# Low parts of weights by a negated copy and an accumulating DMA

## The chip, the core and the metric

The kernel runs on one core of a Trainium2 chip. Its engines run side by side, each with its own queue of instructions, and wait for each other by semaphores: TensorE (PE, with its weight loads PEld), VectorE (DVE), ScalarE (ACT), GpSimd (POOL), and SyncE (SP), which here issues nearly all DMAs. The metric is the device time of one execution in microseconds (us).

## What is computed

One layer of a decoder in float32: 512 tokens with 16 meta tokens ahead of them (528 rows of width 1024). An attention mixer with an indexer that keeps the 128 best keys of each query, a residual with LayerNorm, a SwiGLU feed-forward of width 2816, and a second residual with LayerNorm:

```
proj = h @ w_in                      # q, k, v, indexer
... top-k keys of each query, 16 heads of softmax attention ...
h = layer_norm(alpha*h + out @ w_o, ln1)
ffn = (silu(h @ w_gate) * (h @ w_up)) @ w_down
h = layer_norm(alpha*h + ffn, ln2)
```

The output is h without the meta rows.

## The kernel before

**High and low parts.** PE multiplies in a format with fewer bits than float32. So each float32 operand x is written as hi + lo: hi is x rounded by a ScalarE copy (line 156), lo = x - hi a subtraction (line 159), and a product takes three matmuls, hi·hi, hi·lo and lo·hi (`mm3`, lines 286 to 288; for the down and output weights lines 1063 and 771). Weights are cut so at run time, in chunks of 128 x 1024 (512 KB).

**Chunks.** A chunk passes through three kinds of buffer of three each (`CHUNKS`): raw (`r_wq`, `r_wg`, ...: where SP's load lands), high (`h_...`) and low (`l_...`). `load` issues the DMA, `cut` issues the copy and the subtraction, `chunk` fetches the two parts for the matmuls, and `ahead(name)` cuts the next chunk of the list and loads the two after it. The lists are `g_in` (indexer), `g_qk` (wq0, wk0, ... wq7, wk7, wo0 to wo3, wr0 to wr3) and `g_ff` (wg0, wu0, ... wg21, wu21, then the down chunks wd).

**Late chunks.** `cut(..., late=True)` doesn't issue the subtraction at once but owes it in two pieces: columns 0 to 639 to VectorE, the rest to GpSimd. `settle` issues what is owed, at fixed places of a head, or when `chunk` wants the chunk. Late are fourteen chunks: wq3 to wq7, wk3 to wk7, wo0 to wo2 (cut by `stream`) and wo3. For gate and up, the gate's subtraction is on VectorE and the up's on GpSimd (wg0's is on GpSimd too), the down's on VectorE.

**Order.** The program order of each engine is that of the code. After the indexer and the top-k search comes a loop over the 16 attention heads. In a head stand the scores (`a1S` and so on, lines 313 and 314), VectorE's masked logits with the bias (line 653), ScalarE's exponentials (line 661), GpSimd's normalisation (line 670) and the bias additions for the next head (line 644, `bm`), PE's transposes (line 696), and the products with the values (line 726). Between them `fill` spends a budget of microseconds on pieces of the projections of later heads (`p_q`, `p_k`, lines 286 to 288) and, at the end, of the output projection (line 771). At the end of a head, and twice more within head 0, `stream` cuts the next weight chunk and loads ahead. Then come the first LayerNorm (lines 933 to 976), gate and up (line 991 on: 24 matmuls of 512 columns for each chunk, `p_wg` and `p_wu`), the down product (line 1037 on) and the second LayerNorm.

Of the kernel before, what the change touches and what calls it, by code (L numbers as in the profile page):

```python
# [11 lines left out]
F32 = mybir.dt.float32  # L12
F32R = mybir.dt.float32r
AF = mybir.ActivationFunctionType
ALU = mybir.AluOpType
# [35 lines left out]
AHEAD = 2  # L51
# [66 lines left out]
def trunk(ctx, tc, a, out):  # L118
    nc = tc.nc
# [8 lines left out]
    def unit(name, dt=F32, tag="u"):  # L128
        return up.tile([P, UNIT], dt, name=name, tag=tag, bufs=UNITS[tag])
# [25 lines left out]
    def act_copy(o, i, scale=1.0):  # L155
        nc.scalar.activation(o, i, AF.Copy, scale=scale)  # L156

    def sub(eng, o, x, y):
        eng.tensor_tensor(out=o, in0=x, in1=y.bitcast(F32), op=ALU.subtract)  # L159
# [21 lines left out]
    loaded, split, owed = {}, {}, []  # L181

    def load(group, i):
        if i < len(group):
            nm, src, n, _ = group[i]
            if nm not in loaded:
                loaded[nm] = raw(f"r_{nm}")[:, :n]
                nc.sync.dma_start(loaded[nm], src)

    def cut(group, i, late=False):  # L190
        if i < len(group):
            nm, _, n, eng = group[i]
            if nm not in split:
                load(group, i)
                hi = wp.tile([P, 1024], F32R, name=f"h_{nm}", tag="whi", bufs=CHUNKS[1])[:, :n]
                lo = wp.tile([P, 1024], F32R, name=f"l_{nm}", tag="wlo", bufs=CHUNKS[2])[:, :n]
                act_copy(hi, loaded[nm])
                split[nm] = (hi, lo)
                if late:
                    for e, c0, c1 in ((nc.vector, 0, SHARE), (nc.gpsimd, SHARE, n)):  # L200
                        owed.append((e, lo[:, c0:c1], loaded[nm][:, c0:c1], hi[:, c0:c1]))
                else:
                    sub(ENG[eng], lo, loaded[nm], hi)
# [7 lines left out]
    def chunk(name):  # L211

        group, i = where[name]
        if name not in split:
            cut(group, i)
        settle()
        return split[name]

    def ahead(name, late=False):
        group, i = where[name]  # L220
        cut(group, i + 1, late)
        for j in range(2, AHEAD + 2):
            load(group, i + j)

    def rows_load(name, src, tag="u"):
# [13 lines left out]
    g_in, g_qk, g_ff = groups  # L239
# [121 lines left out]
    for k in range(KT):  # L361
# [10 lines left out]
        if k == 0:  # L372
            load(g_in, 2)
    cut(g_in, 2)
    load(g_in, 3)
    for i, (t0, t1) in enumerate(HALF):
# [185 lines left out]
    def pair(p):  # L562

        pq = bank(f"p_q{p}", "mm")
        steps = project(f"wq{p}", NM, T, pq)
        using[0] = f"wq{p}"
        if p < 2:
            ahead(f"wq{p}")
        for k, _ in enumerate(steps):
            if k < KT - 1:  # L570
                yield 0.65
        Q2[2 * p], Q2[2 * p + 1] = queries(pq, -0.125, [f"q{2 * p + j}" for j in range(2)])
        yield 0.65
        ka = [unit(f"ka{2 * p + j}", F32R, "kq") for j in range(2)]
        for i, (t0, t1) in enumerate(HALF):
            pk = bank(f"p_k{p}_{i}", "mm")
            steps = project(f"wk{p}", t0, t1, pk[:, :264])
            if i == 0:
                using[0] = f"wk{p}"
                if p < 2:  # L580
                    ahead(f"wk{p}")
            for k, _ in enumerate(steps):
                if k < KT - 1:
                    yield 0.33
            keys(pk, t0, t1, *ka)
            if i:
                for j in range(2):
                    KA[2 * p + j], KB[2 * p + j] = ka[j], swapped(ka[j], f"kb{2 * p + j}")
            yield 0.33
# [39 lines left out]
    repeat(16)  # L629
    early(1)  # L630
    ahead("wk1")
    repeat(32)
    cut(g_qk, where["wk2"][1])
# [357 lines left out]
    for f in range(NF):  # L991
# [14 lines left out]
        if f < 8:  # L1006
            if f % 4 == 0:
                hq.append((quad(f"hh{f}", S), quad(f"hl{f}", S)))
            hi, lo = (x[:, f % 4] for x in hq[f // 4])
        else:  # L1010
            hi, lo = unit(f"hh{f}", F32R)[:, :S], unit(f"hl{f}", F32R)[:, :S]
# [25 lines left out]
    for th in range(2):  # L1037
# [9 lines left out]
        for f, o in steps:  # L1047
# [7 lines left out]
            else:  # L1055
                wh, wl = last[f - NF + TAIL]
                if th == 0 and o == outs[0] and f < NF - 1:
                    i = where["wd1_0"][1] + f - NF + TAIL
# [11 lines left out]
            su, n = done[b]  # L1070
# [74 lines left out]
```

## Time and profile before

| | |
|---|---|
| median of 3 runs | 689.28 us (687.64 to 690.19) |
| profiled execution | 688.74 us, its span 687.0 us |
| PE, PEld busy | 97%, 82% of the span |
| DVE, ACT, POOL busy | 61%, 42%, 36% |
| DMA | 83.11 MB, mean 121 GB/s |

Stages in the span: to about 50 us the indexer's projections, to 130 the top-k search beside projections, to 280 the attention heads, to 312 the output projection and first LayerNorm, to 556 gate and up, then the down product and its LayerNorm. Engines overlap, so an engine's busy time counts only where another engine waits for it; a matmul's own duration is modelled and longer than the distance to the next one.

### The profile page before, as it was taken

The numbers are of one execution on the slowest core, as the hardware profiler recorded it, in microseconds if no ns is written. First come the engines' busy times: TensorE is split into PE (matmuls) and PEld (weight loads), VectorE is DVE, ScalarE is ACT, GpSimd is POOL, SyncE is SP. The second block draws the span as 40 slices with busy tenths as digits, with TensorE's granted clock in tenths as the row PEclk, the third lists the DMA queues.
The fourth block names the chain that finished last, engine by engine and source line by source line (L and its number), as shares of the span: only waits on it lengthen the run. The fifth ranks groups of instructions, "written<-read, shape, count | busy, mean of one in ns | idle before, by whom it ended". The sixth has DMA issues, their size and how long they took to land.

```text
span 687.0 us, 9443 instructions
## 1 busy us (share of the span) xinstructions
PE 668.5 (97%) x3440; PEld 564.2 (82%) x3440; DVE 418.3 (61%) x788; ACT 287.6 (42%) x516; POOL 244.8 (36%) x249
## 2 busy tenths in 40 slices
PE   7999999999999999999999999999999999999995
PEld 5888787888998888888888888888888888888884
DVE  5589897898888887686334233343433355575425
ACT  5573512567767675513323233232322344423310
POOL 2063802597786776654212122221212200011004
PEclk9999999999999999999999999999999999999998
DMA  6557131542223245410131322313132267745601
GB/s 235 172 167 253 42 75 37 153 139 79 71 85 109 71 135 189 154 61 29 65 122 62 124 80 104 119 66 123 63 121 90 94 231 234 238 148 198 208 32 61
DMA packets 31806, 83.11 MB, mean 121 GB/s; under 512 B 3744, under 2 KB 8912, under 8 KB 31760
## 3 DMA queue, kind: packets, MB, share of 16 engines
q1 hardware_dynamic: 31328, 82.12, 36.6%
q8 instruction: 27, 0.44, 0.3%
q10 hardware_dynamic: 432, 0.39, 0.2%
q14 instruction: 19, 0.16, 0.1%
HBM read 74.86 MB, written 5.27 MB: 117 GB/s over the span
## 4 chain that ended last, share of the span: by engine, by line
PE 85%; DVE 6%; POOL 3%; ACT 2%; issue 2%; DMA 1%; SPq 0%; POOLq 0%; DVEq 0%; ACTq 0%
PE pd L1063 17%; PE p_wu L287 6%; PE p_wu L286 6%; PE p_wu L288 6%; PE p_wg L287 6%; PE p_wg L286 6%; PE p_wg L288 6%; PE po L771 3%; PE av L726 3%; PE pv L288 2%; PE pv L286 2%; PE pv L287 2%; PE pt L696 2%; PE p_q L288 2%; PE p_q L287 2%
## 5 line engine op out<-in xcount | busy, mean ns | idle before, releaser
L159 POOL TENSOR_TENSOR l_wu<-r_wu,h_wu 128x1024 fp32r<-128x1024 f32 x22 | 52.9, 2405 | 179.5 <-ACT h_wu L156 179.5
L1005 DVE TENSOR_TENSOR sg<-p_wu,sg 128x512 f32<-128x512 f32 x22 | 15.2, 692 | 107.6 <-PE p_wu L288 107.6
L159 DVE TENSOR_TENSOR l_wd<-r_wd,h_wd 128x1024 fp32r<-128x1024 f32 x36 | 45.4, 1263 | 41.2 <-ACT h_wd L156 41.1
L287 PE MATMUL p_wg<-h1l,h_wg 128*128 128x512 f32 (+1 forms) x184 | 70.0, 380 | 0.3 <-DVE h1l L159 0.3
L286 PE MATMUL p_wg<-h1h,h_wg 128*128 128x512 f32 (+1 forms) x184 | 70.0, 381 | 0.0
L286 PE MATMUL p_wu<-h1h,h_wu 128*128 128x512 f32 (+1 forms) x184 | 70.0, 380 | 0.0
L288 PE MATMUL p_wu<-h1h,l_wu 128*128 128x512 f32 (+1 forms) x184 | 69.9, 380 | 0.0
L287 PE MATMUL p_wu<-h1l,h_wu 128*128 128x512 f32 (+1 forms) x184 | 69.9, 380 | 0.0
L288 PE MATMUL p_wg<-h1h,l_wg 128*128 128x512 f32 (+1 forms) x184 | 69.9, 380 | 0.0
L159 DVE TENSOR_TENSOR l_wg<-r_wg,h_wg 128x1024 fp32r<-128x1024 f32 x21 | 52.9, 2518 | 24.4 <-ACT h_wg L156 24.4
L156 ACT ACTIVATE hh<-sg 128x512 fp32r<-128x512 f32 x22 | 13.9, 633 | 119.7 <-DVE sg L1005 119.7
L670 POOL TENSOR_TENSOR lg<-lg,rec 128x144 f32<-128x144 f32 (+1 forms) x64 | 52.6, 846 | 21.9 <-DVE rec L668 21.1
L1063 PE MATMUL pd<-h_wd,hh 128*128 128x512 f32 (+1 forms) x162 | 59.6, 368 | 0.0
L1063 PE MATMUL pd<-h_wd,hl 128*128 128x512 f32 (+1 forms) x162 | 59.6, 368 | 0.0
L1063 PE MATMUL pd<-l_wd,hh 128*128 128x512 f32 (+1 forms) x162 | 59.5, 368 | 0.0
L156 ACT ACTIVATE h_wd<-r_wd 128x1024 fp32r<-128x1024 f32 x36 | 38.1, 1061 | 45.6 <-DMA r_wd<-in_wd 23.2
L644 POOL TENSOR_TENSOR bm<-score,tz 128x256 f32<-128x256 f32 (+1 forms) x64 | 43.9, 717 | 16.4 <-DVE mn L653 14.9
L938 POOL TENSOR_TENSOR fr<-fr,half_neg 128x1 f32<-128x1 f32 x4 | 4.0, 992 | 116.0 <-DVE fr L937 116.0
L661 ACT ACTIVATE lg<-lg,mn 128x272 f32<-128x272 f32 (+1 forms) x64 | 36.3, 571 | 11.6 <-DVE mn L653 11.6
L287 PEld LDWEIGHTS p_wg<-h1l,h_wg 128*128 128x128 f32 x184 | 34.6, 188 | 7.0 <-DVE h1l L159 0.5
L286 PEld LDWEIGHTS p_wg<-h1h,h_wg 128*128 128x128 f32 x184 | 34.6, 188 | 6.9 <-ACT h1h L156 0.2
L288 PEld LDWEIGHTS p_wu<-h1h,l_wu 128*128 128x128 f32 x184 | 34.6, 188 | 6.6
(333 smaller groups left out, 1759.4 us busy)
## 6 DMA issues: line engine op xcount, KB each, us to landing
r_wd<-in_wd SPq DMA_DIRECT2D x36, 512.0 KB, 4.2
r_wg<-in_wg SPq DMA_DIRECT2D x22, 512.0 KB, 3.7
r_wu<-in_wu SPq DMA_DIRECT2D x22, 512.0 KB, 4.5
kb<-ka SPq DMA_DIRECT2D x32, 132.0 KB, 2.3
r_wq<-in_wq SPq DMA_DIRECT2D x8, 512.0 KB, 4.8
r_wk<-in_wk SPq DMA_DIRECT2D x8, 512.0 KB, 3.4
rbig<-rdram SPq DMA_DIRECT2D x1, 3072.0 KB, 15.2
hTr<-in_hT SPq DMA_DIRECT2D x8, 264.0 KB, 5.2
```

Of the source, the lines that this page charges most:

```text
L156: nc.scalar.activation(o, i, AF.Copy, scale=scale)
L159: eng.tensor_tensor(out=o, in0=x, in1=y.bitcast(F32), op=ALU.subtract)
L286: nc.tensor.matmul(o, lh, rh, start=i == 0, stop=False)
L287: nc.tensor.matmul(o, lh, rl, start=False, stop=False)
L288: nc.tensor.matmul(o, ll, rh, start=False, stop=i == KT - 1)
L644: nc.gpsimd.tensor_tensor(out=bm.at(b, W[b] - n, W[b]), in0=mask.at(b, W[b] - n, W[b]), in1=tzs[h][:, 256 - n :], op=ALU.add)
L661: nc.scalar.activation(lg.blk(b), lg.blk(b), AF.Exp, bias=mn[:, i : i + 1], scale=-1.0, accum_out=den[:, b : b + 1])
L670: nc.gpsimd.tensor_tensor(out=lg.blk(b), in0=lg.blk(b), in1=rec[:, b : b + 1].to_broadcast([P, W[b]]), op=ALU.mult)
L726: nc.tensor.matmul(av[:, 512 - w :], lhs, x[:, c : c + w], start=u == 0 and z == 0, stop=u == 4 and z == len(pr) - 1,)
L771: nc.tensor.matmul(po[hf, b], l[:, bs], r, start=k == 0 and i == 0, stop=k == KT - 1 and i == 2)
L1005: nc.vector.tensor_tensor(out=sg, in0=pg[1], in1=sg, op=ALU.mult)
L1063: nc.tensor.matmul(pd[o], l[:, bs], r[:, c0:c1], start=f == 0 and i == 0, stop=f == NF - 1 and i == 2)
```

## The change

Every late attention chunk, and every chunk of gate and up, now gets its low part without a subtraction: ScalarE copies hi, then writes -hi into the low buffer (a second copy with scale -1), and a DMA issued by GpSimd, with an add in it, reads x from the raw buffer and adds it to the low buffer in place. `ahead` now cuts two chunks ahead for gate and up, and loads the two after those.

```
@@ cut @@
                 act_copy(hi, loaded[nm])
                 split[nm] = (hi, lo)
-                if late:
+                if group is g_ff and nm[1] != "d" or late:
+
+                    act_copy(lo, hi.bitcast(F32), scale=-1.0)
+                    nc.gpsimd.dma_start(lo.bitcast(F32), loaded[nm], accum_op=ALU.add)
+                elif late:
                     for e, c0, c1 in ((nc.vector, 0, SHARE), (nc.gpsimd, SHARE, n)):
                         owed.append((e, lo[:, c0:c1], loaded[nm][:, c0:c1], hi[:, c0:c1]))
                 else:
@@ ahead @@
         group, i = where[name]
-        cut(group, i + 1, late)
-        for j in range(2, AHEAD + 2):
+        n = 2 if name[:2] in ("wg", "wu") else 1
+        for j in range(1, n + 1):
+            cut(group, i + j, late)
+        for j in range(n + 1, n + AHEAD + 1):
             load(group, i + j)
```

GpSimd at the end of head 0, before: the last normalisations (`lg`) and the four bias additions for head 1 (`bm`), GpSimd's pieces of wq3 (`l_wq_1429`) and wk3, then the additions for head 2.

```order
L670 TENSOR_TENSOR lg_1367<-lg_1367,rec_1418 128x528
L644 TENSOR_TENSOR bm_638<-score_268,tz_1200 128x256
L644 TENSOR_TENSOR bm_638<-score_268,tz_1200 128x144
L644 TENSOR_TENSOR bm_640<-score_270,tz_1200 128x256
L644 TENSOR_TENSOR bm_639<-score_269,tz_1200 128x256
L159 TENSOR_TENSOR l_wq_1429<-r_wq_1255,h_wq_1428 128x384
L159 TENSOR_TENSOR l_wk_1479<-r_wk_1431,h_wk_1478 128x384
L644 TENSOR_TENSOR bm_638<-score_268,tz_1375 128x256
```

The same place after:

```order
L676 TENSOR_TENSOR lg_1367<-lg_1367,rec_1418 128x528
L650 TENSOR_TENSOR bm_638<-score_268,tz_1200 128x256
L650 TENSOR_TENSOR bm_638<-score_268,tz_1200 128x144
L650 TENSOR_TENSOR bm_640<-score_270,tz_1200 128x256
L650 TENSOR_TENSOR bm_639<-score_269,tz_1200 128x256
L202 DMA l_wq_1429<-r_wq_1255 128x1024
L202 DMA l_wk_1479<-r_wk_1433 128x1024
L202 DMA l_wq_1512<-r_wq_1435 128x1024
L650 TENSOR_TENSOR bm_638<-score_268,tz_1375 128x256
```

Three DMA issues stand where the two pieces stood, and they now carry all 1024 columns. PE at the same place, after, with what each instruction waits for (`DMASW` is the semaphore of a DMA issued by GpSimd; before, the third of these rows waited for `DVE`):

```order
L292 MATMUL p_q_1504<-hTh_77,h_wq_1428 128x512 [waits DVE_49,PE_49,Activation_49]
L293 MATMUL p_q_1504<-hTl_78,h_wq_1428 128x512
L294 MATMUL p_q_1504<-hTh_77,l_wq_1429 128x512 [waits DMASW0_49]
L292 MATMUL p_q_1504<-hTh_77,h_wq_1428 128x512
L293 MATMUL p_q_1504<-hTl_78,h_wq_1428 128x512
L294 MATMUL p_q_1504<-hTh_77,l_wq_1429 128x512
L319 MATMUL a1S_1518<-ka_915,q_909 128x272
```

PE's own order is unchanged: two pieces of wq3's projection stand ahead of the scores of head 1 (`a1S`). ScalarE at the start of gate and up, before: the last LayerNorm copies (`h1h`), the high part of wg1, the first silu (`sg`, `hh`), then wu1 and wg2.

```order
L156 ACTIVATE h1h_3561<-tz_3800 128x4x128
L156 ACTIVATE h_wg_3842<-r_wg_3585 128x1024
L1004 ACT_TABLE_LOAD
L1004 ACTIVATE sg_3872<-p_wg_3738 128x512
L156 ACTIVATE hh_3875<-sg_3872 128x512
L156 ACTIVATE h_wu_3881<-r_wu_3816 128x1024
L156 ACTIVATE h_wg_3911<-r_wg_3846 128x1024
```

After:

```order
L156 ACTIVATE h1h_3563<-tz_3802 128x4x128
L156 ACTIVATE h_wg_3818<-r_wg_3587 128x1024
L156 ACTIVATE l_wg_3819<-h_wg_3818 128x1024
L156 ACTIVATE h_wu_3851<-r_wu_3823 128x1024
L156 ACTIVATE l_wu_3852<-h_wu_3851 128x1024
L1010 ACT_TABLE_LOAD
L1010 ACTIVATE sg_3882<-p_wg_3740 128x512
L156 ACTIVATE hh_3885<-sg_3882 128x512
L156 ACTIVATE h_wg_3891<-r_wg_3825 128x1024
```

Each high part is followed by the negated copy into the low buffer, and wu1 has moved ahead of the silu.

## Rows read from the trace of the kernel before

**Rows 1.** Page: busy us of the engines, and PE's share in 40 slices

```profile
PE 668.5 (97%) x3440; PEld 564.2 (82%) x3440; DVE 418.3 (61%) x788; ACT 287.6 (42%) x516; POOL 244.8 (36%) x249
...
PE   7999999999999999999999999999999999999995
```

**Rows 2.** Page: the chain that ended last, by engine

```profile
PE 85%; DVE 6%; POOL 3%; ACT 2%; issue 2%; DMA 1%; SPq 0%; POOLq 0%; DVEq 0%; ACTq 0%
```

**Rows 3.** Stretches: length, busy PE, PEld, DVE, ACT, POOL, clock, DMA share, GB/s

```profile
165.00:200.00 35.00, 34.59 (x236) 31.56 (x235) 31.42 (x86) 25.87 (x65) 26.99 (x35) 1.00 0.37 108
400.00:500.00 100.00, 100.00 (x443) 82.81 (x442) 35.74 (x27) 28.20 (x36) 21.68 (x9) 1.00 0.29 101
```

**Rows 4.** PE's waits from 147 to 300: total us, times, longest

```profile
PE p_k L286 <- DVE q L329: 1.3, 1, 1.3
PE pt L696 <- POOL lg L670: 0.9, 1, 0.9
PE pt L696 <- DVE ptl L159: 0.9, 3, 0.4
```

**Rows 5.** Timeline around 135 to 143: start, us, engine, line, [idle before <- releaser]

```profile
135.24 1.04 ACT L156 ACTIVATE h_wq<-r_wq 128x1024 fp32r<-128x1024 f32 x1
...
138.04 1.14 DVE L159 TENSOR_TENSOR l_wq<-r_wq,h_wq 128x640 fp32r<-128x640 f32 x1
...
138.45 3.76 POOL L644 TENSOR_TENSOR bm<-score,tz 128x256 f32<-128x256 f32 x4
...
139.23 0.51 PE L288 MATMUL p_q<-hTh,l_wq 128*128 128x512 f32 x1 [0.17 <-DVE l_wq L159]
...
142.16 1.02 POOL L159 TENSOR_TENSOR l_wq<-r_wq,h_wq 128x384 fp32r<-128x384 f32 x1
```

**Rows 6.** Groups by form, bias additions: busy us, mean ns, idle before

```profile
L644 POOL TENSOR_TENSOR bm<-score,tz 128x256 f32<-128x256 f32 x48 | 36.5, 776 | 16.4 <-DVE mn L653 14.9 <-DMA tz<-rbig 1.0 <-DVE score L505 0.4
```

**Rows 7.** Page: DMA issues: KB each, median us from issue to landing

```profile
kb<-ka SPq DMA_DIRECT2D x32, 132.0 KB, 2.3
...
r_wk<-in_wk SPq DMA_DIRECT2D x8, 512.0 KB, 3.4
rbig<-rdram SPq DMA_DIRECT2D x1, 3072.0 KB, 15.2
```

**Rows 8.** Stretches at the start and the end, columns as rows 3

```profile
8.00:10.00 2.00, 1.60 (x10) 1.58 (x10) 2.00 (x4) 1.83 (x4) 0.91 (x2) 0.74 1.05 402
10.00:12.00 2.00, 2.00 (x9) 1.62 (x8) 2.00 (x4) 1.90 (x4) 0.21 (x1) 0.50 1.06 409
12.00:15.00 3.00, 3.00 (x19) 2.65 (x19) 2.04 (x4) 1.82 (x3) 0.98 (x2) 0.94 0.50 191
678.00:680.00 2.00, 0.37 (x4) 0.16 (x2) 1.86 (x7) 0.00 (x0) 1.92 (x2) 1.00 0.02 6
680.00:682.00 2.00, 0.00 (x0) 0.00 (x0) 1.56 (x3) 0.00 (x0) 1.90 (x3) 0.85 0.35 131
```

**Rows 9.** Tile l_wq on VectorE: ns least/median/most, first and last start

```profile
L159 DVE TENSOR_TENSOR l_wq<-r_wq,h_wq x5: 795/799/1273, 138.0 to 217.1; 128x640 fp32r<-128x640 f32 x5
```

**Rows 10.** Timeline, chunk wo2: its copy, GpSimd's piece, first use on PE

```profile
251.03 1.05 ACT L156 ACTIVATE h_wo<-r_wo 128x1024 fp32r<-128x1024 f32 x1
...
257.23 1.01 POOL L159 TENSOR_TENSOR l_wo<-r_wo,h_wo 128x384 fp32r<-128x384 f32 x1
...
263.25 0.40 PE L771 MATMUL po<-l_wo,ath 128*128 128x512 f32 x1
```

**Rows 11.** Timeline in gate and up: copies of ScalarE, first low-part uses on PE

```profile
321.47 1.05 ACT L156 ACTIVATE h_wg<-r_wg 128x1024 fp32r<-128x1024 f32 x1
...
328.08 0.39 PE L288 MATMUL p_wg<-h1h,l_wg 128*128 128x512 f32 x1
...
340.05 1.05 ACT L156 ACTIVATE h_wu<-r_wu 128x1024 fp32r<-128x1024 f32 x1
...
349.86 0.39 PE L288 MATMUL p_wg<-h1h,l_wg 128*128 128x512 f32 x1
```

## The prediction

> **What bounds the kernel now.** I began with the page's busy times: PE is busy 97% of the span and every slice but the first and the last reads 9 [rows 1]. The chain that ended last says the same: 85% of it is PE, 6% VectorE, 3% GpSimd, 2% ScalarE [rows 2]. A change that touches only ScalarE, VectorE, GpSimd and the DMA engines can therefore gain no more than what PE still waits for, and loses what it makes PE wait for. So I asked stage by stage. In the FFN (400 to 500 us) PE is busy 100.00 of 100 us and VectorE 35.74, GpSimd 21.68: all 44 subtractions of gate and up lie under matmuls [rows 3]. In the attention heads (165 to 200 us) VectorE is busy 31.42 of 35 us and GpSimd 26.99, but PE still 34.59 [rows 3]. Over all heads and the output projection (147 to 300 us) the three longest kinds of PE wait sum to 3.1 us: 1.3 on the query's low part (DVE q), 0.9 on GpSimd's normalised logits, 0.9 on ptl [rows 4]. That is what there is to win.
>
> **Part 1: wq3, the first late chunk.** This is the term that decides. wq3 is split and used within head 0, with no head between. Before, ScalarE makes its high part at 135.24, VectorE starts the low part's first 640 columns at 138.04, and PE takes the first low block at 139.23, having idled 0.17 us for it: just in time [rows 5]. GpSimd's share, columns 640 to 1023, comes only at 142.16, behind the four bias additions that begin at 138.45 and take 3.76 us [rows 5]; that was no harm, since PE needs those columns several blocks later. After the change the whole low part, first columns included, is made by a DMA that GpSimd issues, and in its program this DMA stands behind the same four additions, while on PE the matmul stands where it stood and now waits for the DMA's semaphore. In PE's order the scores of head 1 come four matmuls later, so everything else waits with it.
>
> When does it land? The additions lose their competitor on VectorE (the l_wq and l_wk subtractions leave), so I take 0.78 us each [rows 6], 3.1 together: GpSimd is free at 141.5. ScalarE is no limit: 135.24 plus two copies of 1.04 is 137.3. From issue to landing no row shows an accumulating DMA. Nearest are plain ones: 132 KB from SBUF to SBUF land in 2.3 us, a 512 KB load in 3.4, 3072 KB in 15.2 [rows 7]. The accumulating one moves 512 KB but must also read its target. My lower end is a plain 512 KB, 3.4. The line through the two larger rows is (15.2 - 3.4)/(3072 - 512) = 0.0046 us a KB; 1024 KB on it gives 3.4 + 2.4 = 5.8, and 1536 KB (two reads and a write each counted in full) 8.1, my upper end. I take 5.8, an estimate from these rows, with the second read counted and the write beside it. So it lands at 141.5 + 5.8 = 147.3, and PE stands for 147.3 - 139.2 = **8.1 us** (5.7 with the lower end, 10.4 with the upper).
>
> The Trainium skill, "DMA: Bandwidth & Descriptors", section "Anatomy of one DMA — SWDGE (gpsimd) path", fits 2.0 us plus bytes over 436 GB/s, 3.2 us for a plain 512 KB, near the 3.4 of the row; "Collectives: The Full Stack", section on the bandwidth ceiling, says that an adding transfer costs double because it reads two sources, which makes it 4.4. By the pages the stall would be 6.7 and the whole sum 1.4 us less than mine. No run here yet shows it.
>
> **Part 2: the clock after that stall.** PE's last work ends at 678.4 (0.37 us in the slice from 678), and the slice from 680 has a mean of 0.85, so the clock went to 1.2 GHz 3.0 us after PE fell idle. At the start the slices 8 to 15 read 0.74, 0.50 and 0.94, which is 1.0 + 2.0 + 0.4 = 3.4 us at 1.2 GHz while PE was at work [rows 8]. A stall of 8 us is longer than those 3.0, so I expect PE to resume at 1.2 GHz and to run there for up to 3.4 us, losing half of it: **1.7 us** (ends: 0 and twice that).
>
> **Part 3: the other twelve late attention chunks and wo3.** Each loses a VectorE subtraction of 0.80 us [rows 9] and a GpSimd one of 1.0 [rows 5], and gains a ScalarE copy of 1.05 and a DMA issue on GpSimd. They have time: the tightest I found is wo2, copied at 251.03 and its low part first used at 263.25; two copies end at 253.1, so 10.1 us remain for the DMA [rows 10]. SP's queue waits too: its next weight load needs the raw buffer that the DMA reads, and behind it stand the key swaps and bias rows for heads two or more away; an extra 4 us is covered. Bias additions queue behind each DMA issue, which itself waits for ScalarE's second copy; they would wait for that head's logits anyway. Of PE's 3.1 us of waits, the 0.9 on GpSimd should go, since a subtraction of 1.01 us stands right ahead of the normalisation it waited for [rows 10]; of the 0.9 on ptl I take half; but the 1.3 on q ends a run of ScalarE work in a head with a chunk copy, so there the second copy adds 1.05. Net **-0.3 us** (ends -3.1 and +1.0).
>
> **Part 4: gate and up.** Chunks are now split two ahead. In the steady rhythm ScalarE is free for the next gate at 340.05, after hh; high part and negative copy take 2.1 us, to 342.15, and PE asks for that gate's low part (wg3) at 349.86, so the DMA has 7.7 us [rows 11]: covered at 5.8, uncovered at 8.1. The up chunk follows half a period later with more room. The removed subtractions give nothing, since PE never waited there [rows 3]. The first gate so split, wg1, has less: its copy can't start before 321.47, behind the last norm's copies, two copies end at 323.6, and PE uses it at 328.08, leaving 4.5 us [rows 11]. At 5.8 that is a wait of **1.3 us** (0 and 3.6 at the ends). wg0 and wu0 are split some 25 us before use, and the down weights are split as before.
>
> **Sum.** 8.1 + 1.7 - 0.3 + 1.3 = 10.8 us on the profiled execution's own 688.74, which is 0.5 under the median of the three timed runs, 689.28. Against that median: 689.28 + 10.8 = **700**.
>
> **Rivals.** (a) The accumulation is as quick as a plain load and the freed engines pay: stall 5.7, no slow clock, wg1 on time, all three PE waits gone: 5.7 - 3.1 = +2.6, 692. For it: the row of 3.4 us. Against it: a second read and issue by GpSimd's program.
> (b) Faster: the heads are paced by VectorE, not by PE. Then 14 subtractions of 0.80 us come off the heads, 11.2 us, against the smallest stall, 5.7: -5.5, 684. It decides once each head gets shorter by more than 0.4 us. For it: VectorE at 90% there. Against it: PE's waits there are a third of that sum.
> (c) The DMA takes more than 7.7 us, since it competes with a 512 KB weight load per chunk. Then every gate of the FFN waits: at 9 us 20 times 1.3 = 26, with 11.3 at wq3, 3.4 of slow clock and 4.5 at wg1: +45, 734. For it: nothing in the trace shows such a DMA. Against it: 101 GB/s in use in the FFN, far under the 409 seen at 10 to 12 us [rows 3, 8].
>
> **How the numbers follow.** My forecast (the DMA between 4.5 and 7 us) holds 0.64, with a range of its own from 696 to 703; (a) 0.14, (b) 0.07, (c) 0.15. The lower end of the whole range is (a), 691. The upper is a DMA at 8.1 us: 10.4 + 3.4 + 1.0 + 3.6 + 20 x 0.4 = 26, 715, below most of (c). A measurement of this kernel can tell about 0.5% from no change, 685.8 to 692.7: (b) is faster, (a) lies inside, the rest is slower.
>
> **What would show it.** A PE row near 139 us that idles about 8 us on a DMA into l_wq, GpSimd issuing that DMA only after its fourth bias addition, and a granted clock of 0.5 just behind it; a PE wait of about a microsecond at wg1; no PE wait in the later FFN; head to head times hardly shorter. I am wrong if the low part of wq3 lands before 141, if heads shorten by half a microsecond each, or if PE waits at every gate.

## The result, and the profile after

The changed kernel takes 736.48 us (median of 4 runs, 732.38 to 738.63), the kernel before 688.56 beside it (687.64 to 690.19): a ratio of 1.0686 (95% interval 1.065 to 1.0722). Forecast were 700 us and 691 to 715: the sign was right, the size wrong by a factor of four. The profiled execution took 738.23 us, its span 736.4, so 49.4 us of span are to be found.

The page of the kernel after: busy times, PE's share and granted clock in 40 slices, the chain by engine, one group of matmuls, DMA issues.

```profile
PE 684.8 (93%) x3440; PEld 577.7 (78%) x3440; DVE 380.5 (52%) x753; ACT 348.1 (47%) x574; POOL 218.3 (30%) x270
...
PE   7999999598788878889999999999999999999993
...
PEclk9999999999999989999999999999999999999997
...
PE 76%; DVE 7%; ACT 6%; issue 4%; POOL 3%; DMA 3%; SPq 0%; POOLq 0%; DVEq 0%; ACTq 0%
...
L294 PE MATMUL p_wg<-h1h,l_wg 128*128 128x512 f32 (+1 forms) x184 | 70.0, 380 | 0.3 <-DMA l_wg<-r_wg 0.3
...
l_wg<-r_wg POOLq DMA_DIRECT2D x22, 512.0 KB, 4.9
l_wu<-r_wu POOLq DMA_DIRECT2D x22, 512.0 KB, 5.5
```

Against [rows 1, 2]: VectorE and GpSimd are less busy by 38 and 27 us, as the change intends, and PE's chain share falls from 85% to 76%. PE's slices place the loss: one 5 near 140 us, 7 and 8 from about 165 to 330 us, and 9 elsewhere but in the first and the last. So gate and up are not where it went, and the heads are. Stretches of the two kernels say so too (length, busy PE, PEld, DVE, ACT, POOL, clock, DMA share, GB/s):

```profile
144.00:146.00 2.00, 0.00 (x0) 0.00 (x0) 0.00 (x0) 0.31 (x1) 0.96 (x2) 0.52 1.06 197
146.00:148.00 2.00, 1.02 (x2) 0.83 (x3) 0.00 (x0) 0.00 (x0) 0.00 (x0) 0.50 1.05 197
148.00:150.00 2.00, 2.00 (x9) 1.80 (x8) 0.00 (x0) 0.00 (x0) 0.00 (x0) 0.50 1.03 197
150.00:152.00 2.00, 2.00 (x15) 1.96 (x14) 1.78 (x9) 1.00 (x4) 1.35 (x3) 0.78 1.11 133
...
165.00:200.00 35.00, 28.35 (x173) 25.58 (x171) 28.36 (x59) 22.03 (x52) 17.97 (x25) 0.90 0.41 98
400.00:500.00 100.00, 100.00 (x442) 82.79 (x442) 12.46 (x18) 47.93 (x55) 16.32 (x19) 1.00 0.83 195
```

In the same 35 us of heads PE did 236 matmuls before and 173 now, at a clock of 0.90 instead of 1.00; in the FFN it is as full as in [rows 3]. By the starts of the score matmuls and of the first gate and down matmuls, the 49.4 us split into: 1.3 ahead of the heads, 7.3 in head 0, 34.2 in heads 1 to 14, 3.1 from there to the first gate, 0.6 in gate and up, 2.9 from there to the end.

What PE waited for from 125 to 310 us (total us, times, longest):

```profile
PE pt L702 <- DVE ptl L159: 25.3, 11, 2.9
PE p_q L294 <- DMA l_wq<-r_wq: 5.8, 1, 5.8
PE p_k L292 <- DVE q L335: 1.0, 1, 1.0
```

The wait on ptl was 0.9 us in [rows 4] and is 25.3 now. ptl is a VectorE subtraction of ordinary length; what stands ahead of it on VectorE is the low part of the meta rows' weights, `mh` = lg - mh, a small operation that the change doesn't touch. Its tile in the kernel before (ns least/median/most):

```profile
L687 DVE TENSOR_TENSOR mh<-lg,mh x16: 219/650/961, 143.3 to 278.4; 128x64 fp32r<-128x64 f32 x16
```

and after:

```profile
L693 DVE TENSOR_TENSOR mh<-lg,mh x16: 223/3146/3162, 152.2 to 321.0; 128x64 fp32r<-128x64 f32 x16
```

In the ten heads in which a chunk's DMA is issued it takes 3.15 us; in the others 0.22 to 0.66, but 1.27 in the last one. The timeline after shows both places, wq3 and the second of these ten heads (start, duration, engine, line, [idle before <- releaser]):

```profile
136.47 1.04 ACT L156 ACTIVATE h_wq<-r_wq 128x1024 fp32r<-128x1024 f32 x1
137.54 1.06 ACT L156 ACTIVATE l_wq<-h_wq 128x1024 fp32r<-128x1024 f32 x1
...
139.68 2.56 POOL L650 TENSOR_TENSOR bm<-score,tz 128x256 f32<-128x256 f32 x4
142.18 1.02 POOL L202 DMA_DIRECT2D l_wq<-r_wq  x1
...
146.98 0.80 PE L294 MATMUL p_q<-hTh,l_wq 128*128 128x512 f32 x1 [5.81 <-DMA l_wq<-r_wq]
...
180.81 1.05 ACT L156 ACTIVATE h_wq<-r_wq 128x1024 fp32r<-128x1024 f32 x1
181.90 1.06 ACT L156 ACTIVATE l_wq<-h_wq 128x1024 fp32r<-128x1024 f32 x1
182.86 0.51 ACT L667 ACTIVATE lg<-lg,mn 128x272 f32<-128x272 f32 x1
183.26 0.88 POOL L202 DMA_DIRECT2D l_wq<-r_wq  x1 [4.95 <-ACT l_wq L156]
183.64 3.16 DVE L693 TENSOR_TENSOR mh<-lg,mh 128x64 fp32r<-128x64 f32 x1 [0.16 <-ACT mh L156]
183.87 2.84 POOL L650 TENSOR_TENSOR bm<-score,tz 128x256 f32<-128x256 f32 x4
186.73 1.27 DVE L159 TENSOR_TENSOR ptl<-pt,pt 128x512 fp32r<-128x512 f32 x2
187.46 0.44 PE L702 MATMUL pt<-ident,lg 128*128 128x128 f32 x2 [2.18 <-DVE ptl L159]
```

Read the second half from the top. ScalarE now makes two copies of the chunk, and behind them stand the exponentials (`lg`), that is 1.06 us later. GpSimd, its queue in order, has waited 4.95 us for the second copy; the bias additions (`bm`), ready long before (in the kernel before they ran beside the logits), stand behind that DMA issue, and so begin only at 183.87. `mh`, whose start is recorded at 183.64, doesn't end until all four additions are through, 0.09 us after the last. That is 2.5 us on VectorE ahead of ptl, in ten heads. At wq3 the clock stood at 1.2 GHz for 6.8 us, 144.1 to 150.9 (the windows above read 0.50). The first 2.9 of them lie inside PE's wait, which ends at 146.98, so PE worked at 1.2 GHz for 3.9 us. It stood there for 3.4 us at the end of, or just behind, eight of the ten long waits on ptl, as in the head shown:

```profile
189.00:191.00 2.00, 2.00 (x11) 2.00 (x11) 1.69 (x4) 0.00 (x0) 1.45 (x3) 0.50 0.84 305
```

In the 3.1 us ahead of the first gate PE waits once more, 2.0 us in the last head's products (first line). The chain that ended last shows why (start, us, what): the DMA into wo3's low part holds its raw buffer until 324.06, only then does SP issue the next weight load (`r_wr`), and ScalarE's copy of that load (`woh`) stands ahead of the `pt` copy that PE wants.

```profile
PE av L732 <- ACT pt L156: 2.0, 1, 2.0
...
319.52 4.54 DMA l_wo<-r_wo
324.11 3.42 DMA r_wr<-in_wo
327.55 1.06 ACT woh L156
```

### The profile page after: what moved, and what is told of

The parts are those of the page before. It is cut to its first block, busy times and chain, and to the rows that moved or that the text cites. A ratio compares the mean times of both kernels' runs of the same rounds, so it can differ in the third digit from the quotient of the medians.

```text
span 736.4 us, 9562 instructions
## 1 busy us (share of the span) xinstructions
PE 684.8 (93%) x3440; PEld 577.7 (78%) x3440; DVE 380.5 (52%) x753; ACT 348.1 (47%) x574; POOL 218.3 (30%) x270
## 3 DMA queue, kind: packets, MB, share of 16 engines
q1 hardware_dynamic: 31328, 82.12, 34.2%
## 4 chain that ended last, share of the span: by engine, by line
PE 76%; DVE 7%; ACT 6%; issue 4%; POOL 3%; DMA 3%; SPq 0%; POOLq 0%; DVEq 0%; ACTq 0%
PE pd L1069 16%; PE p_wg L294 5%; PE p_wu L292 5%; PE p_wu L293 5%; PE p_wu L294 5%; PE p_wg L292 5%; PE p_wg L293 5%; PE av L732 3%; DVE mh L693 3%; PE po L777 2%; PE pv L294 2%; PE pv L292 2%; PE pv L293 2%; PE p_q L294 2%; PE p_q L293 2%
## 5 line engine op out<-in xcount | busy, mean ns | idle before, releaser
L202 POOL DMA_DIRECT2D l_wg<-r_wg x22 | 19.0, 865 | 127.9 <-ACT l_wg L156 97.3
L676 POOL TENSOR_TENSOR lg<-lg,rec 128x144 f32<-128x144 f32 (+1 forms) x64 | 47.0, 762 | 29.7 <-DVE rec L674 25.6
L702 PE MATMUL pt<-ident,lg 128*128 128x128 f32 x160 | 23.7, 279 | 25.3 <-DVE ptl L159 25.3
L702 PEld LDWEIGHTS pt<-ident,lg 128*128 128x128 f32 x160 | 18.6, 141 | 30.0 <-DVE ptl L159 28.7
L156 ACT ACTIVATE h_wu<-r_wu 128x1024 fp32r<-128x1024 f32 x22 | 23.3, 1061 | 37.0 <-PE p_wg L293 34.0
L292 PE MATMUL p_k<-hTh,h_wk 128*128 128x264 f32 x128 | 39.9, 312 | 1.0 <-DVE q L335 1.0
```

The source lines that it names most:

```text
L292: nc.tensor.matmul(o, lh, rh, start=i == 0, stop=False)
L676: nc.gpsimd.tensor_tensor(out=lg.blk(b), in0=lg.blk(b), in1=rec[:, b : b + 1].to_broadcast([P, W[b]]), op=ALU.mult)
L702: nc.tensor.transpose(pt[:, c : c + P], lg.at(b, NM + j * P, NM + (j + 1) * P), ident)
```

## Experiments

Each figure beside "before" is the kernel before, timed in the same job. The kernel after was timed in the first job only, 47.9 us above the kernel before of that job, which was 1.0 to 1.6 us slower there than in the later ones. So what an experiment gives back is counted as 47.9 less its own distance from the kernel before.

**1. The DMAs where the subtractions stood.** The late attention chunks' DMAs are owed and issued by `settle`, behind the bias additions; the two ScalarE copies stay.

```
+                    if late:
+                        owed.append((nc.gpsimd, lo, loaded[nm], None))
+                    else:
+                        nc.gpsimd.dma_start(lo.bitcast(F32), loaded[nm], accum_op=ALU.add)
...
+            if x[3] is None:
+                nc.gpsimd.dma_start(x[1].bitcast(F32), x[2], accum_op=ALU.add)
```

> The DMAs of the late attention chunks are issued where GpSimd's subtractions stood before (behind the normalisations of the next head), the two ScalarE copies stay. Port theory (in ten heads the four bias additions run as one block behind a late DMA issue, and VectorE's subtraction into mh, which reads two SBUF tiles, is held for the whole block, 3.15 us instead of 0.65): mh back to about 0.65 in all heads, PE's wait on ptl from 25 to under 4 us, total 698 to 708. ScalarE theory (the second copy delays the exponentials and mh, GpSimd's order is incidental): mh stays near 3, total over 725.

Measured: 712.96 us (711.3 to 714.62; before 687.0), ratio 1.0375 [1.0316, 1.0434]. `mh` is back at 0.22 to 0.66 us in all heads but the last, and the wait on ptl falls from 25.3 to 2.3. So the place of the DMA issue in GpSimd's program, not the second copy, makes the 3.15 us. The total is above the 698 to 708 expected. PE now waits for a low part of the output weights, and at wq3 the clock stays at 1.2 GHz for 10.2 us instead of 6.8:

```profile
PE po L783 <- DMA l_wo<-r_wo: 4.6, 1, 4.6
```

And its timeline shows the same hold on another operation, a subtraction with two SBUF operands that falls behind a DMA issue:

```profile
193.58 0.87 POOL L216 DMA_DIRECT2D l_wk<-r_wk  x1
...
194.19 2.17 POOL L682 TENSOR_TENSOR lg<-lg,rec 128x400 f32<-128x400 f32 x2
194.21 2.71 DVE L159 TENSOR_TENSOR atl<-att,ath 128x512 fp32r<-128x512 f32 x1
```

`atl` takes 2.71 us here and ends 0.56 after both normalisations (196.36), so nearly all of its undisturbed 0.68 us lies behind them; in heads of this kernel where it doesn't fall behind an issue it takes 0.68 to 1.61.

**2. A subtraction in the DMA's place.** The kernel before, with the negated copy, and GpSimd's 384-column subtraction put where the DMA stands in the kernel after; no DMA is issued by GpSimd.

```
-                    for e, c0, c1 in ((nc.vector, 0, SHARE), (nc.gpsimd, SHARE, n)):
+                    act_copy(lo, hi.bitcast(F32), scale=-1.0)
+                    sub(nc.gpsimd, lo[:, SHARE:], loaded[nm][:, SHARE:], hi[:, SHARE:])
+                    for e, c0, c1 in ((nc.vector, 0, SHARE),):
```

> The kernel before, with the negated ScalarE copy added and GpSimd's 384-column subtraction issued at once, in the place where the changed kernel issues its DMA; no accumulating DMA anywhere, gate and up as before. Port theory: any GpSimd instruction that waits there for ScalarE makes the bias additions late and lets them hold mh: mh near 3 us in about ten heads, total 712 to 728. DMA theory (writing the descriptors on GpSimd is what holds VectorE): mh near 0.65, total 690 to 700.

Measured: 692.66 us (692.29 to 694.81), ratio 1.0092 [1.006, 1.0124]. The additions come late, as after, and follow the operation ahead of them without a pause, and `mh` starts beside the operation ahead of them, but gets its turn at that operation's end:

```profile
171.13 1.02 POOL L159 TENSOR_TENSOR l_wq<-r_wq,h_wq 128x384 fp32r<-128x384 f32 x1 [2.33 <-ACT l_wq L156]
171.74 0.50 DVE L689 TENSOR_TENSOR mh<-lg,mh 128x64 fp32r<-128x64 f32 x1
172.11 3.22 POOL L646 TENSOR_TENSOR bm<-score,tz 128x256 f32<-128x256 f32 x4
```

`mh` ends at 172.24, 0.09 after the subtraction. That sank the first theory, that late additions alone hold VectorE. The time is the one that the other theory expected, that the issue itself holds it; experiment 5 takes that one away.

**3. A plain DMA and no negated copy** in the late attention chunks. Their low parts hold x itself: the kernel leaves out the subtraction of hi, which the layer needs.

```
-                    act_copy(lo, hi.bitcast(F32), scale=-1.0)
-                    nc.gpsimd.dma_start(lo.bitcast(F32), loaded[nm], accum_op=ALU.add)
+                    if not late:
+                        act_copy(lo, hi.bitcast(F32), scale=-1.0)
+                        nc.gpsimd.dma_start(lo.bitcast(F32), loaded[nm], accum_op=ALU.add)
+                    else:
+                        nc.gpsimd.dma_start(lo.bitcast(F32), loaded[nm])
```

> The changed kernel with a plain DMA in place of the accumulating one for the late attention chunks and no negated copy there (their low parts hold x itself); the DMA no longer waits for ScalarE. Port theory: GpSimd issues it before the next head begins, the bias additions start on time, mh near 0.65, total 696 to 706 (wq3's stall stays). DMA theory: mh near 3 us in ten heads, total over 722.

Measured: 697.67 us (696.86 to 698.49), ratio 1.0153 [1.0122, 1.0183]. Without the copy to wait for, the DMA is issued earlier, the additions are early again, and the median `mh` is 0.66. Fourteen pairs of subtractions are gone, and heads 1 to 14 take 128.0 us from scores to scores, against 127.4 before. One head is shorter, head 14, by 1.0 us, since the 0.9 of PE's wait on GpSimd's lg is gone; the others make up for it. So freeing VectorE and GpSimd doesn't shorten the heads as a whole. wq3 still costs:

```profile
PE p_q L297 <- DMA l_wq<-r_wq: 5.1, 1, 5.1
```

**4. The second copy alone.** The kernel before, with the negated copy written and then overwritten by the subtractions.

```
+                    act_copy(lo, hi.bitcast(F32), scale=-1.0)
```

> The kernel before, with the negated ScalarE copy added for every late attention chunk (its result is overwritten by the subtractions, which stay). Port theory: mh unchanged near 0.65; the copy costs at most 1.06 us in each of ten heads, total 690 to 699. ScalarE theory: most of the loss shows here, total over 712.

Measured: 692.55 us (692.45 to 692.65; before 687.0), ratio 1.0078 [1.0049, 1.0107]: fourteen copies of 1.06 us on ScalarE cost 5.6 us (3.4 to 7.4 by the interval), under half their length, but more than the 1.05 that Part 3 gave them. Experiment 2 has the same copies and costs the same, so they account for its loss.

**5. The additions moved.** The kernel after, with the four bias additions behind the first two normalisations; DMA issue and copies stay.

```
-            if h:
-                bias(h + 1)
...
         if 0 < h < H:
             normalise(h, now[0], now[2], (0, 1))
+            bias(h + 1)
```

> The changed kernel with the four bias additions of every head moved behind the first two normalisations, so that nothing on GpSimd follows a DMA issue at once. Theory now (a two-input VectorE subtraction that starts while GpSimd issues an accumulating DMA is held until GpSimd's unbroken run of work behind it ends): mh in the ten heads ends with the DMA issue, 0.4 to 0.6 us, and no mh of 3.1. Rival (mh is held by the additions themselves, wherever they stand, or by the DMA's transfer of some 4 us): mh stays over 2 us. Total: about 25 us below the changed kernel's 736 if the later normalisations cost nothing, so 708 to 728.

Measured: 710.94 us (710.28 to 711.6; before 687.11), ratio 1.0343 [1.0316, 1.037]: 24.1 us come back. The timeline:

```profile
176.23 0.88 POOL L202 DMA_DIRECT2D l_wq<-r_wq  x1 [0.87 <-PE pt L702]
...
176.61 0.23 DVE L693 TENSOR_TENSOR mh<-lg,mh 128x64 fp32r<-128x64 f32 x1 [0.16 <-ACT mh L156]
```

`mh` runs beside the DMA issue in 0.23 us. So neither the issue nor the transfer holds VectorE: it takes the issue with ready additions directly behind it. The additions now delay the normalisations behind them (PE waits 5.2 us in all on GpSimd's lg), so the move isn't free.

**6. `mh` ahead of the logits** in the kernel after.

```
+            if h:
+                meta_parts(h - 1, last)
             now = logits(h, banks, range(5) if h else (2, 0, 4, 1, 3))
...
-            meta_parts(h - 1, last)
+            if h == H:
+                meta_parts(h - 1, last)
```

> The changed kernel with the parts of the meta keys (mh, on ScalarE and VectorE) made ahead of the head's logits instead of behind them, so that VectorE asks for mh before GpSimd's DMA issue. Theory: mh under 0.7 us in all heads, no long wait for ptl, total 704 to 716. Rival (the second ScalarE copy sets the head's length): head to head still over 12 us, total over 725. New cost that it may bring: mh now waits for the previous head's last normalisation and holds up the logits.

Measured: 714.26 us (713.64 to 714.88), ratio 1.0391 [1.0364, 1.0418]. `mh` takes 0.22 us, away from the DMA issue, in all heads but the last, and 20.8 us come back; 9.2 us of waits on ptl stay. So the long `mh` is a cause of the wait on ptl, not just beside it.

**7. wq3 by subtractions** in the kernel after.

```
-                if group is g_ff and nm[1] != "d" or late:
+                if group is g_ff and nm[1] != "d" or late and nm != "wq3":
```

> The changed kernel with wq3 alone made by the old subtractions on VectorE and GpSimd. Theory: PE's 5.8 us wait at wq3 and the 6.8 us at 1.2 GHz behind it go, mh stays at 3.15 in ten heads: 736 - 5.8 - 3.4 = 727, 724 to 730. Rival (the stall was absorbed later, since the heads are held up anyway): 733 to 737.

Measured: 725.43 us (two runs, 723.17 and 727.7; before 687.11), ratio 1.0554 [1.0508, 1.06]: 9.6 us come back, of which the trace places 7.4 in head 0 (15.8 us instead of 23.2). Stall and slow stretch at wq3 are gone, `mh` stays (median 3.11 us), and so does the wait:

```profile
PE pt L702 <- DVE ptl L159: 22.5, 9, 2.9
```

**8. Gate and up alone** by the accumulating DMA; attention as before.

```
-                if group is g_ff and nm[1] != "d" or late:
+                if group is g_ff and nm[1] != "d":
```

> The negated copy and accumulating DMA for gate and up alone (with the cuts two ahead); the late attention chunks as before. Theory: PE still never waits in the FFN, so the same as before within 0.3% (686 to 690), in spite of 44 subtractions fewer on VectorE and GpSimd. Rival (the FFN pays for the doubled DMA traffic): over 692.

Measured: 690.08 us (8 runs, 689.24 to 691.53; before 687.11), ratio 1.0043 [1.0029, 1.0057]. PE is full in the FFN as before:

```profile
400.00:500.00 100.00, 100.00 (x442) 82.80 (x442) 12.46 (x18) 47.24 (x54) 16.08 (x19) 1.00 0.83 191
```

The time is just above the 686 to 690 expected. From first gate to first down matmul it takes 244.3 us against 243.7. The rest of the 3.0 us lies largely behind the last work: GpSimd's last operation ends at 683.23 in a span of 687.7, so 4.5 us remain, and 2.7 in the kernel before.

**9. Two additions instead of four** right behind the DMA issue in the kernel after, the other two behind the first two normalisations.

```
-                bias(h + 1)
+                bias(h + 1, (1, 0))
...
+            bias(h + 1, (3, 2))
```

> The changed kernel, with only two of a head's four bias additions right behind the DMA issue, and the other two moved behind the first two normalisations. Run theory (behind a DMA issue VectorE's mh gets its turn only when the whole run of ready GpSimd operations is through): in the ten heads with a DMA mh takes 1.7 to 1.8 us instead of 3.15, to the end of the second addition, and the kernel about 736 - 10 x 1.4 = 722. Rival (the DMA itself, its issue or its transfer, holds VectorE for about 3 us): mh stays at 3.1. Rival (the hold needs a long queue behind the issue): mh at 0.65 or less, and 711 as with all four moved.

Measured: 714.88 us (one run; before 687.6). The run theory gave 1.7 to 1.8 us for `mh`; in nine of the ten heads it is 1.78 to 1.80, and in one, where it starts later, 1.26, each to 0.1 us after the second addition:

```profile
178.98 0.88 POOL L202 DMA_DIRECT2D l_wq<-r_wq  x1 [1.58 <-ACT l_wq L156]
179.36 1.80 DVE L693 TENSOR_TENSOR mh<-lg,mh 128x64 fp32r<-128x64 f32 x1 [0.16 <-ACT mh L156]
179.59 1.48 POOL L650 TENSOR_TENSOR bm<-score,tz 128x256 f32<-128x256 f32 x2
```

The hold is as long as the run of ready operations. The total is 7 us under the 722 expected: the waits on ptl are now 1.5 us at most, and behind them the clock no longer falls: longer waits had cost more than their length.

**10. The three harms taken out.** DMAs as in experiment 1, wq3 and wo3 by subtractions.

```
+                if group is g_ff and nm[1] != "d" or late and nm not in ("wq3", "wo3"):
```

> The changed kernel with the three harms that the earlier runs named taken out: the accumulating DMAs of late attention chunks stand where the subtractions stood (behind the bias additions), and wq3 and wo3, whose low parts are wanted at once, keep their subtractions. If the harms add up: 712.8 less the stall and slow clock of wq3 (5.8 + 5.1) and the wait at wo3 (4.6) = 697; what is left over the kernel before is then the second ScalarE copy (5) and the DMAs of gate and up (3). If they don't add up, because the next wait stands right behind each: 702 to 708. If the freed VectorE and GpSimd time pays at last: under 689.

Measured: 702.95 us (701.89 to 704.05; before 687.6), ratio 1.022 [1.0205, 1.0236], in the 702 to 708 expected if the harms don't just add up. Above the 5.6 of the second copy and the 3.0 of gate and up, 6.8 remain. The wait on the output weights stayed:

```profile
PE po L783 <- DMA l_wo<-r_wo: 3.8, 1, 3.8
```

So it was never wo3's, as I had read it in experiment 1 and written in the expectation, but wo2's, the third chunk. Its DMA is issued at 263.16 and PE goes on at 272.20. The DMA issues from 255 to 275 us (KB each, us to landing):

```profile
l_wo<-r_wo POOLq DMA_DIRECT2D x1, 512.0 KB, 9.0
...
y<-in_x SPq DMA_DIRECT2D x8, 256.0 KB, 5.4
```

It lands in 9.0 us instead of 4.5, beside the loads of the residual that SP issues at this time (8 x 256 KB). The head that holds this wait, with 3.4 us at 1.2 GHz behind it, is 4.3 us longer than in experiment 4. One other, with 3.4 us at 1.2 GHz from 160.1, is 3.4 longer: PE waits there 1.9 us in all on GpSimd's lg, which stands behind additions that waited for a bias row (`tz`) from SP's queue:

```profile
154.61 2.59 POOL L656 TENSOR_TENSOR bm<-score,tz 128x256 f32<-128x256 f32 x4 [6.32 <-DMA tz<-rbig]
```

The two heads cover the 6.8. The 3.1 us ahead of the first gate are gone, where wo3 keeps its subtractions (44.8 us from the scores of head 15 to the first gate, 44.8 before, 47.9 after).

**11. `mh` ahead of the logits in the kernel before**, the same edit as experiment 6, as a possible gain of its own.

> The kernel before, with mh made ahead of the logits in each head: no low part changes. If VectorE's mh (0.65 us there, against 0.22 without GpSimd beside it) were worth anything in the kernel before, 15 x 0.4 = 6 us less, 683; if PE covers it, 688 as before; if the logits behind it come late, as in the changed kernel with the same edit, up to 9 us of new waits on ptl, 697.

Measured: 689.42 us (8 runs, 688.62 to 691.55; before 687.6), ratio 1.0028 [1.0013, 1.0042]. `mh` falls to a median of 0.23 us and PE gets nothing from it. No version tried here beats the kernel before.

## Why the prediction was wrong

**The step that failed** is in Part 3: "Bias additions queue behind each DMA issue, which itself waits for ScalarE's second copy; they would wait for that head's logits anyway." The first half named the place exactly. The second looked only at who reads the additions' results, and nobody is late there, indeed. It didn't ask what else the additions do when they run later: before, they ran mostly beside the logits; now they start when VectorE makes `mh`, and hold it for their whole run. Part 3 came to -0.3 us (at worst +1.0). Moving the additions alone gives back 24.1 us (experiment 5), against 10 x (3.15 - 0.65) = 25.0 by the rows. That the two are so near is partly luck: the 25.0 leave out the falls of the clock, eight in the heads after and two in experiment 5, and experiment 5 brings 5.2 us of waits on lg of its own.

Two more terms of Part 3 were too small. The second copy, costed at 1.05 in one head, takes 5.6 (experiment 4); that it stands ahead of the exponentials that PE's transposes need is the likely reason, argued from the order. And "an extra 4 us is covered", said of SP's queue, doesn't hold at wo3: `r_wr` is issued at 324.11, right behind the landing of l_wo, and costs 3.1 us ahead of the first gate.

**Part 1** had the mechanism and erred in the sizes. Forecast was a stall of 8.1 us, a DMA of 5.8, and data at 147.3; measured 5.81, 4.8 (142.18 to 146.98) and 147.0. The landing came out right by two errors, an issue 0.7 later (the additions ahead of it began 1.2 later and took 2.6, not 3.1) and a DMA 1.0 shorter; PE came to the wait 1.9 later than taken from [rows 5], 1.3 of it because the head began later. [rows 7] took 3.4 us for a 512 KB load, the quickest of the five kinds on the page before; the others have 3.7 to 4.8. The Trainium skill's doubling of an adding transfer ("Collectives: The Full Stack", section on the bandwidth ceiling), which gave 4.4 us here, is nearer to the medians of the attention chunks and of gate, 4.5 to 4.9 us, than the 5.8 of the line that I drew through the loads; the 5.5 of up is nearer to the line. A DMA of 4.4 us fits the 4.5 left at wg1 too, so by the pages the sum would have been 2.7 us less, not 1.4.

**Part 2** was right at wq3: 1.7 us were forecast for 3.4 us of work at 1.2 GHz, and it was 3.9, so 2.0 lost. Stall and clock together, 7.8 us by the rows, 7.3 by the length of head 0 and 9.6 by experiment 7, were forecast as 9.8; only the stall was too long. What it left out is the clock in the heads, eight falls of 3.4 us behind waits of 2.2 to 2.9, shorter than the 3.0 that it took from [rows 8]; experiment 5 has two, so six falls fewer are part of the 24.1.

**Part 4** was right: no wait at a gate, with a DMA of 4.9 us in a room of 7.7; wg1 waits 0.3 us, within its ends 0 and 3.6. Not foreseen was the end of the program.

**The sum**, by experiments: 24.1 (additions) + 9.6 (wq3) + 5.6 (second copy) + 3.0 (gate and up, and the end) = 42.3 of the 47.9 us between the medians, and the 3.1 ahead of the first gate by the traces make it 45.4. The other 2.5 weren't tested apart. That the parts add up at all isn't a given, as experiment 10 shows; the four runs of the kernel after alone lie 6 us apart.

**The rivals.** (a) and (b) fell. Of the three PE waits that were to go, the 0.9 on GpSimd's lg and the 1.3 on q are gone, the second only in the longer heads (in experiment 3 it is 1.3 again); the 1.0 on q above is another one, at 136.67, which was 1.05 before, at 135.45, outside the stretch of [rows 4]. The third, on ptl, grew to 25.3. Experiment 3 shows that without the subtractions the heads as a whole aren't shorter. Rival (c) gave 734, close to the result, but for a reason that isn't there: no gate waits. A number that fits confirmed nothing here; PE's slices, full from 400 to 500 us, refuted it at once. (The range's lower end, 691, is (a)'s 691.9 cut off, where (a) itself says 692.)

**What stays open** is why VectorE isn't let in between the additions of such a run. One difference is seen: directly behind a DMA issue each GpSimd operation of the run is recorded as starting 0.31 to 0.34 us before the one ahead of it ends (30 of 30 in the kernel after; 183.87 + 2.84 above is the sum of four such), while in the other runs of additions that is about 0.04. In experiments 1 and 3 some additions stand directly behind a DMA issue in GpSimd's program but begin only 0.7 us or more after it; they overlap by 0.05 at most, and `mh` takes 0.4 to 0.7. So it takes additions that wait already when the issue runs. That the overlap is the cause is argued, not shown, and whether the issue of a plain DMA with ready additions behind it does the same wasn't tried.

## What to carry to other kernels

When a step makes another engine's operations start later, ask not only who waits for their results but what they now run beside: an operation of three tenths of a microsecond on the path can wait for a whole run of work that nobody is waiting for. Don't put the issue of a GpSimd DMA, above all one that waits, ahead of ready GpSimd work in its queue. And ask what a transfer still reads when it takes the place of an instruction: the buffer comes free later, and so does the next load. Work taken off engines that PE doesn't wait for gained nothing here, while a wait of two to three microseconds on PE cost its length and, in eight of ten, 3.4 us at half the clock.

## What the runs showed of the hardware

- **VectorE behind GpSimd.** `mh`, two SBUF operands, 0.22 us alone, waits to the end of the GpSimd operation in progress (0.50 us, experiment 2), and behind a DMA issue to the end of the whole run that is ready: two operations 1.80, four 3.15 us. The Trainium skill, "SBUF — State Buffer", section "Who interferes with whom", says that such a VectorE operation and a GpSimd one that reads SBUF exclude each other for one whole instruction, whichever comes first. The 0.50 us agree; the 3.15 and 1.80 us don't, and there the measurement decides.
- **An accumulating DMA within SBUF**, 512 KB, issued by GpSimd: 0.87 us of GpSimd's time for the issue, 4.5 to 5.5 us to land in the medians of the kinds of chunk, 6.6 and 8.9 for the two issued right behind wq3's, and 9.0 us beside 2 MB of loads (experiment 10). The quickest takes 4.5, the quickest plain one of the same size 2.9 (experiment 3). Rival (c) named the competition; in the FFN no gate took more than 6.7 us in the kernel after, under the 7.7 that it had.
- **The end of a program with GpSimd DMAs.** From GpSimd's last operation to the span's end: 2.7 us without one (before, experiment 2), 4.5 us with 44 (experiment 8), 5.6 us with 58, here in the kernel after, in a span of 736.4:

```profile
730.12 0.72 POOL L949 TENSOR_TENSOR y<-y,b 128x256 f32<-128x256 f32 x1
```

- **The clock.** In the kernel after it was granted at 1.2 GHz for 3.4 us with eight of ten waits of 2.2 to 2.9 us on PE, and for 6.8 us from 2.9 us into one of 5.8. The waits on ptl of up to 1.5 us in experiment 9 had no such stretch, but a wait of 1.4 us with one of 0.7 close behind it had (experiment 5, from 273.4), and so had four waits of 0.3 to 0.7 within 3 us (experiment 10, from 160.1). So the length of a single wait doesn't decide it.
